# One more step between VectorE's softplus and the triangular products of a stick-breaking head

## The chip, the cores and the metric

The kernel runs on one core of a Trainium2 chip. The metric is the device time of one execution in microseconds (us); lower is better. The engines are TensorE (PE in the trace; PEld is its weight load), VectorE (DVE), ScalarE (ACT), GpSimd (POOL) and SyncE (SP, which here issues most DMAs). Each engine takes its instructions from a queue of its own in the order of the program and waits where data or a buffer is missing.

## The reference

A decoder layer for 512 tokens of width 2048: a mixer with two groups of eight heads each, then a mixture of 32 experts. Group A is sparse attention, group B is stick-breaking attention. What a head of group B computes:

```python
z = einsum('bqhd,bshd->bhqs', q_blk, k)
log_1m = where(strict, log_sigmoid(-z), 0.0)
tail = cumsum(log_1m, axis=3, reverse=True) - log_1m
a = where(strict, exp(log_sigmoid(z) + tail), 0.0)
o = einsum('bhqs,bshd->bqhd', a, v)
```

The outputs of both groups are normed over their heads, concatenated and projected (`w_out`); the result is gated by a modulation vector and added to the residual stream. The experts follow on the normed residual, with the router's two choices per token.

## The kernel before

All weights are streamed from memory. A pool of 23 buffers in SBUF (`big`, tag `b`) serves nearly everything: weight chunks as loaded, their split into a high and a low half (`hl`, ScalarE writes the high half and VectorE, in one stage GpSimd, the low one, L380-L381), modulation rows, heads. Eight banks of PSUM are used as four for the main projections (`mm`) and four for all else (`at`).

The first half of the kernel runs a main stream of projections: for group B the names are B0, B1 (q), B2, B3 (k), B4, B5 (v), two of each with four heads in each; Q0 to Q3 are projections for group A. `steps` (L907) walks a projection in groups of products (`main_b`, L621: six products of 512 columns to a group), and the output projection `main_o` (L966) does the same in six segments O0 to O5; the first two cover group A's heads in the columns 0 and 1, the third is the first that reads group B's.

Everything else is written as generators and put in four lanes (`Lanes`, L49). After each group of main products `tick(rate)` gives every lane `rate` steps in turn (`RATES`, L43: B4, Q2 and Q3 1.2, B5 0.6, segment O0 0.95, segment O1 0.2); a step runs one generator up to its next `yield`. That fixes the order of instructions in every engine's queue: a `yield` issues nothing, it only lets one round of the other lanes and main products come ahead. Where a result is needed, `lanes.until` turns the lanes with no main products between; L1061 does so ahead of the third output segment until group B's norm has been issued.

`stick` (L782) is a head of group B. It works in three blocks of keys, (2,3), (1,) and (0,). A block: the score products into a PSUM bank (L795-L796), step; three activations of ScalarE, |z|, exp, ln (L799-L801), step; VectorE's maximum and sum, the softplus e (L803), step; the triangular products, which add minus the running sums of e to the bank (L806-L811), with GpSimd keeping the total `tot` (L807, L813, L815), step; ScalarE's last exp, which frees the bank (L817), step. That is 15 steps a head. `stick_pv` (L821) multiplies by v later, frees the head's buffer and collects squares for the norm. `sticks` (L844) opens heads as `room` allows: heads 0 to 3 run in lanes 2 and 3 beside B4, Q2 and Q3; heads 4 to 6 start in lanes 3, 0 and 2 at the end of B3 and run beside B5; head 7 follows in lane 3. `norm_o(1)` (L858, L872-L892) is group B's norm: it waits for all heads, adds the squares, sums over partitions with a product (`on`), takes the reciprocal root (`rstd`, L148), and then scales (L888) and splits (ScalarE's high part, L892's low part) the eight heads.

`mod_chunk` (L271) accumulates modulation rows on VectorE (L269, 2.3 us each) between the chunks of weights, and `mod_done` (L330) turns the finished ones with a few products.

Of the kernel before, what the change touches and what calls it, by code (L numbers as in the profile page):

```python
# [75 lines left out]
def tile_hybrid_layer(ctx: ExitStack, tc, A, out, dbg=None):  # L76
# [9 lines left out]
    def slot(shape, dt=F32, name="b"):  # L86
        t = big.tile(shape, dt, name=name, tag="b")
        return t

    def bank(tag, name, dt=F32):  # L90
        t = ps.tile([P, 512], dt, name=name, tag=tag)
        return t
# [3 lines left out]
    def act(o, i, f=AF.Copy, **kw):  # L96
        return SC.activation(o, i, f, **kw)  # L97

    def mm(o, l, r, start, stop, skip=False):
        return T.matmul(o, l, r, start=start, stop=stop, skip_group_check=skip)  # L100
# [681 lines left out]
    def stick(h):  # L782
        g, hh = divmod(h, 4)
        q, k = qb[g], kb[g]
        opened[0] += 1
        buf = slot([P, 1664], name="st")
        tot = buf[:, 1152:1664]
        for js in ((2, 3), (1,), (0,)):
            o = pk[js[0]].start
            at = {j: slice(pk[j].start - o, pk[j].stop - o) for j in js}  # L790
            n = at[js[-1]].stop
            z = bank("at", "z")[:, :n]
            for j in js:
                zj = z[:, at[j]]
                mm(zj, k[:, hh, 128 * j:128 * j + 128], q[:, hh, 128 * j:], j == js[0], False, True)  # L795
                mm(zj[:, 0:128], identb, smaskb, False, False, True)  # L796
            yield
            e = buf[:, o:o + n]
            act(e, z, AF.Abs)  # L799
            act(e, e, AF.Exp, scale=-1.0)  # L800
            act(e, e, AF.Ln, bias=one1)  # L801
            yield
            V.scalar_tensor_tensor(e, z, 0.0, e, op0=OP.max, op1=OP.add)  # L803
            yield
            if js == (2, 3):
                mm(z[:, 128:256], mones, e[:, 256:384], False, False, True)  # L806
                G.tensor_tensor(tot[:, 384:], e[:, 128:256], e[:, 256:384], op=OP.add)  # L807
            else:
                mm(z[:, 128:], mones, tot[:, 128 * js[0] + 128:], False, False, True)
            for j in js:  # L810
                mm(z[:, at[j]], negU, e[:, at[j]], False, j == js[-1], True)  # L811
            if js == (1,):
                G.tensor_tensor(tot[:, 256:], tot[:, 256:], e[:, 128:], op=OP.add)  # L813
            if js[0]:
                G.tensor_copy(tot[:, 128 * js[0]:128 * js[0] + 128], e[:, 0:128])  # L815
            yield
            act(e, z, AF.Exp)  # L817
            yield
        weighed.append((h, buf))
# [24 lines left out]
    def sticks(left=0):  # L844

        while stick_left[0] > left:
            if weighed and vb_done[weighed[0][0] // 4]:
                yield from stick_pv(*weighed.pop(0))
            elif len(todo) > left and opened[0] < room() and kb_done[todo[0] // 4] and qb_done[todo[0] // 4]:
                yield from stick(todo.pop(0))  # L850
            else:
                yield
# [699 lines left out]
```

## Time and profile before

| | us |
|---|---|
| median of 3 runs | 1876.78 |
| lowest, highest | 1874.24, 1879.22 |
| profiled execution | 1876.25 |
| its span, first to last instruction | 1874.4 |

| engine | busy us | share of the span |
|---|---|---|
| TensorE | 1735.2 | 93% |
| VectorE | 938.9 | 50% |
| ScalarE | 507.6 | 27% |
| GpSimd | 153.2 | 8% |

The span is that of one execution on the chip. A row of a timeline gives the start, the duration of the row's instructions (several of one kind are merged, x2) and in brackets how long the engine had stood idle before and what released it. A releaser is inferred from semaphores: it is the last thing that was waited for, not always the first cause.

### The profile page before, as it was taken

What the parts mean: (1) busy time and instruction counts of PE and PEld (TensorE: products, weight loads), DVE (VectorE), ACT (ScalarE), POOL (GpSimd) and SP (SyncE); (2) the same over time, 40 slices, a digit from 0 to 9 for tenths busy, and PEclk for the clock granted to TensorE, in tenths of its full rate; (3) what the DMA queues carried; (4) which work ended last, traced back from release to release, by engine and by line L of the source; (5) the groups of instructions that cost most, each with busy time, mean ns of one, the idle gap of its engine ahead of it and who ended that gap; (6) DMA issues with size and microseconds to landing.
All of it is one profiled execution on the core that took longest, in us unless ns stands there. A gap on an engine that the chain in (4) does not pass through costs nothing.

```text
span 1874.4 us, 20840 instructions
## 1 busy us (share of the span) xinstructions
PE 1735.2 (93%) x8097; PEld 975.6 (52%) x8097; DVE 938.9 (50%) x1518; ACT 507.6 (27%) x960; POOL 153.2 (8%) x116
## 2 busy tenths in 40 slices
PE   6999997999899998998899999999999999999997
PEld 3777775775567676887333333333333333333333
DVE  6798943378955857555334424342434233333425
ACT  4323342555455532321212111121112110211010
POOL 0001010332225110000100000000000000000000
PEclk8999998999999999999999999999999999999999
DMA  9876734312245645669899999999999999999997
GB/s 389 339 279 229 257 125 156 135 68 84 74 138 201 230 179 205 222 225 409 313 412 419 419 420 420 419 419 420 420 419 419 420 419 420 419 420 419 419 413 275
DMA packets 91574, 585.06 MB, mean 312 GB/s; under 512 B 10866, under 2 KB 11034, under 8 KB 27046
## 3 DMA queue, kind: packets, MB, share of 16 engines
q1 hardware_dynamic: 87184, 569.09, 76.0%
q0 software_dynamic: 4288, 14.60, 2.1%
q8 instruction: 65, 1.06, 0.2%
q14 instruction: 37, 0.30, 0.0%
HBM read 583.64 MB, written 8.40 MB: 316 GB/s over the span
## 4 chain that ended last, share of the span: by engine, by line
DMA 41%; PE 36%; DVE 14%; issue 4%; ACT 4%; POOL 1%; SPq 0%; DVEq 0%; ACTq 0%; POOLq 0%
DMA w_u<-in_w_up 15%; DMA w_g<-in_w_gate 12%; DMA w_d<-in_w_down 12%; PE O L100 8%; PE B L100 7%; PE y L100 3%; PE u L100 3%; PE Q L100 2%; PE g L100 2%; PE z L100 2%; DVE accv L269 2%; DVE acc L269 1%; PE cb L100 1%; DVE sel L722 1%; DMA w_m<-in_w_m 1%
## 5 line engine op out<-in xcount | busy, mean ns | idle before, releaser
L100 PE MATMUL u<-w_u,xe 128*64 128x512 f32 x1024 | 267.3, 605 | 22.8 <-DMA w_u<-in_w_up 21.6
L100 PE MATMUL g<-w_g,xe 128*64 128x512 f32 x1024 | 240.8, 596 | 18.2 <-DMA w_g<-in_w_gate 18.0
L1277 DVE TENSOR_TENSOR x<-cb,x 128x512 f32<-128x512 f32 x256 | 157.2, 681 | 186.2 <-PE cb L100 186.2
L100 PE MATMUL y<-w_d,uT 128*64 128x512 f32 x1024 | 236.9, 600 | 0.7 <-ACT uT L97 0.7
L100 PEld LDWEIGHTS u<-w_u,xe 128*64 128x64 f32 x1024 | 78.4, 138 | 200.9 <-issue 137.7
L100 PEld LDWEIGHTS g<-w_g,xe 128*64 128x64 f32 x1024 | 75.9, 137 | 170.5 <-issue 130.7
L269 DVE SCALAR_TENSOR_TENSOR accv<-w_m_None,sil,accv 128x2048 f32<-128x2048 f32 x62 | 150.4, 2426 | 6.7 <-DMA accv<-in_b_gate 6.5
L1267 DVE SCALAR_TENSOR_TENSOR yt<-y,gs,accv 128x512 f32<-128x512 f32 x64 | 47.8, 747 | 200.4 <-PE y L100 200.4
L97 ACT ACTIVATE xe<-ga,modc 128x128 f32<-128x128 f32 x254 | 93.9, 463 | 126.2 <-PE y L100 95.7
L100 PEld LDWEIGHTS y<-w_d,uT 128*64 128x64 f32 x1024 | 66.5, 136 | 116.0 <-issue 107.6
L100 PE MATMUL cb<-yH,oT 128*128 128x512 f32 x256 | 107.7, 421 | 0.9 <-DVE x L1277 0.9
L97 ACT ACTIVATE uT<-uT 128x512 f32<-128x512 f32 x16 | 9.6, 598 | 343.5 <-PE uT L1318 343.5
L100 PE MATMUL cb<-yL,oT 128*128 128x512 f32 x256 | 101.0, 394 | 0.0
L1269 DVE TENSOR_TENSOR yL<-yt,yH 128x512 fp32r<-128x512 f32 x64 | 44.3, 692 | 110.3 <-DMA w_g<-in_w_gate 52.7
L97 ACT ACTIVATE yH<-yt 128x512 fp32r<-128x512 f32 x64 | 40.3, 630 | 204.6 <-DVE yt L1267 121.4
L1219 POOL DMA_INDIRECT xg<-x1d,gi x15 | 15.2, 1014 | 818.7 <-DVE t L1222 597.2
L100 PEld LDWEIGHTS cb<-yH,oT 128*128 128x128 f32 x256 | 48.0, 188 | 49.8 <-issue 38.9
L1241 PEld LDWEIGHTS ga<-cst,xg 128*128 128x128 f32 x252 | 35.2, 209 | 62.9 <-issue 42.0
L97 ACT ACTIVATE hl<-w_B 128x1024 fp32r<-128x1024 f32 x48 | 50.5, 1052 | 54.9 <-DVE accv L269 29.5
L1312 DVE TENSOR_TENSOR u<-sg,u 128x512 f32<-128x512 f32 x16 | 11.0, 688 | 106.0 <-PE u L100 106.0
L381 DVE TENSOR_TENSOR hl<-w_O,hl 128x1024 fp32r<-128x1024 f32 x32 | 39.2, 1229 | 43.6 <-ACT hl L97 28.3
L381 POOL TENSOR_TENSOR hl<-w_B,hl 128x1024 fp32r<-128x1024 f32 x17 | 47.9, 2817 | 142.6 <-ACT hl L97 112.3
(428 smaller groups left out, 2915.4 us busy)
## 6 DMA issues: line engine op xcount, KB each, us to landing
w_g<-in_w_gate SPq DMA_DIRECT2D x128, 1024.0 KB, 19.9
w_u<-in_w_up SPq DMA_DIRECT2D x128, 1024.0 KB, 21.2
w_d<-in_w_down SPq DMA_DIRECT2D x128, 1024.0 KB, 19.9
w_m_None<-in_w_mod SPq DMA_DIRECT2D x64, 1024.0 KB, 4.9
w_m<-in_w_m SPq DMA_DIRECT2D x32, 1024.0 KB, 11.7
w_B<-in_w_b SPq DMA_DIRECT2D x48, 512.0 KB, 4.6
w_O<-in_w_o SPq DMA_DIRECT2D x16, 1024.0 KB, 5.0
w_A<-in_w_a SPq DMA_DIRECT2D x8, 848.0 KB, 11.3
```

The lines of the kernel that those rows point to most:

```text
L97: return SC.activation(o, i, f, **kw)
L100: return T.matmul(o, l, r, start=start, stop=stop, skip_group_check=skip)
L269: V.scalar_tensor_tensor(acc, w, s, acc, op0=OP.mult, op1=OP.add)
L381: low_eng[0].tensor_tensor(t[:, 1], s, t[:, 0].bitcast(F32), op=OP.subtract)
L722: V.match_replace(out=acc, in_to_replace=m8, in_values=acc, imm_value=SEL)
L1219: G.indirect_dma_start(xs, None, x1d[:, :], bass.IndirectOffsetOnAxis(ap=gi[:, 0:1], axis=0), bounds_check=S - 1, oob_is_err=False)
L1241: T.transpose(pb[:, 128 * j:128 * j + 128], xs[:, 512 * c:512 * c + 512].rearrange("p (k j) -> p j k", j=4)[:, j], ident)
L1267: V.scalar_tensor_tensor(yt, y, g, rowv[G2][:, cs], op0=OP.mult, op1=OP.mult)
L1269: V.tensor_tensor(yL[:, cs], yt, yH[:, cs].bitcast(F32), op=OP.subtract)
L1277: return lambda: V.tensor_tensor(acc[q][:, t], pb, acc[q][:, t], op=OP.add)
L1312: V.tensor_tensor(u, sg, pb, op=OP.mult)
```

## The change

Between VectorE's softplus and the triangular products a head yields twice instead of once. No instruction is added, removed or altered; a head has 18 steps instead of 15.

```diff
             act(e, e, AF.Ln, bias=one1)
             yield
             V.scalar_tensor_tensor(e, z, 0.0, e, op0=OP.max, op1=OP.add)
+            yield
             yield
             if js == (2, 3):
                 mm(z[:, 128:256], mones, e[:, 256:384], False, False, True)
```

## Rows read from the trace of the kernel before

**Rows 1.** Page, chain that ended last, shares of the span by engine.

```profile
DMA 41%; PE 36%; DVE 14%; issue 4%; ACT 4%; POOL 1%; SPq 0%; DVEq 0%; ACTq 0%; POOLq 0%
```

**Rows 2.** Stretches: us; busy PE, PEld, DVE, ACT, POOL; clock, DMA share, GB/s.

```profile
245.00:330.00 85.00, 74.41 (x417) 54.96 (x416) 33.46 (x32) 29.41 (x49) 13.36 (x14) 0.94 0.41 141
...
577.00:650.00 73.00, 68.38 (x283) 49.44 (x282) 53.38 (x48) 41.44 (x73) 29.72 (x22) 1.00 0.55 203
650.00:712.30 62.30, 58.91 (x239) 44.79 (x238) 38.78 (x43) 23.01 (x34) 4.76 (x5) 0.97 0.55 206
...
853.00:1874.40 1021.40, 951.72 (x4106) 385.84 (x4104) 361.97 (x700) 164.96 (x376) 23.70 (x24) 0.99 0.99 407
```

**Rows 3.** SyncE: a wait of its queue (us, times, longest); first expert load.

```profile
SPq L247 <- PE O L100: 104.1, 20, 10.1
...
852.98 6.47 SPq L247 DMA_DIRECT2D w_g<-in_w_gate  x6
```

**Rows 4.** TensorE's timeline, heads 0-2: start, us, engine, operation, [idle before <- releaser].

```profile
290.79 1.19 PE L100 MATMUL z<-st,mone 128*128 128x256 f32 x2 [3.79 <-DVE st L803]
...
292.49 1.63 PE L100 MATMUL B<-hl,h2H 128*128 128x512 f32 x2
...
303.70 0.88 PE L100 MATMUL z<-st,mone 128*128 128x384 f32 x2 [2.64 <-DVE st L803]
...
325.03 4.58 PE L100 MATMUL pob<-st,B 128*128 128x128 f32 x16 [2.21 <-ACT B L97]
```

**Rows 5.** ScalarE's timeline, same stretch.

```profile
287.04 1.06 ACT L97 ACTIVATE hl<-w_B 128x1024 fp32r<-128x1024 f32 x1 [8.29 <-PE B L100]
```

**Rows 6.** TensorE's timeline, heads 4-6.

```profile
595.33 1.12 PE L100 MATMUL md<-accv,one 128*128 128x512 f32 x2 [1.59 <-ACT st L97]
...
624.95 0.88 PE L100 MATMUL z<-st,mone 128*128 128x384 f32 x2 [0.52 <-DVE st L803]
...
642.94 0.50 PE L100 MATMUL B<-hl,h3H 128*128 128x512 f32 x1 [1.14 <-DVE hl L381]
```

**Rows 7.** VectorE's timeline, end of B5.

```profile
642.80 0.55 DVE L803 SCALAR_TENSOR_TENSOR st<-z,st 128x384 f32<-128x384 f32 x1
...
643.27 4.81 DVE L269 SCALAR_TENSOR_TENSOR accv<-w_m_None,sil,accv 128x2048 f32<-128x2048 f32 x2
...
650.95 2.36 DVE L381 TENSOR_TENSOR hl<-w_O,hl 128x1024 fp32r<-128x1024 f32 x2 [2.86 <-ACT hl L97]
```

**Rows 8.** Tile of a head: one of ScalarE's activations, ns min/median/max.

```profile
L97 ACT ACTIVATE st<-st,one x24: 614/617/727, 248.1 to 667.0; 128x384 f32<-128x384 f32 x16, 128x512 f32<-128x512 f32 x8
```

**Rows 9.** TensorE's timeline, output projection's first segments.

```profile
650.02 2.42 PE L100 MATMUL pob<-st,B 128*128 128x128 f32 x8
...
651.88 1.03 PE L100 MATMUL O<-hl,o00H 128*128 128x512 f32 x2
...
682.98 1.02 PE L100 MATMUL on<-ssb,one 128*128 128x512 f32 x2
...
688.77 1.19 PE L100 MATMUL O<-hl,o00H 128*128 128x512 f32 x2 [3.38 <-DVE mix L1013]
...
712.23 0.70 PE L100 MATMUL O<-hl,o10H 128*128 128x512 f32 x2
...
719.12 0.49 PE L100 MATMUL O<-hl,o10H 128*128 128x512 f32 x1 [1.18 <-ACT hl L97]
...
720.38 0.50 PE L100 MATMUL O<-hl,o10H 128*128 128x512 f32 x1 [0.77 <-DVE hl L381]
```

**Rows 10.** VectorE's timeline, norm of group B (first and last of five).

```profile
685.42 0.69 DVE L153 SCALAR_TENSOR_TENSOR rt<-on,ro 128x512 f32<-128x512 f32 x1 [3.52 <-ACT ro L97]
...
687.94 0.68 DVE L1013 TENSOR_TENSOR mix<-O,accv 128x512 f32<-128x512 f32 x1
...
694.38 1.40 DVE L888 SCALAR_TENSOR_TENSOR B<-B,vecs,ro 128x512 f32<-128x512 f32 x2
...
697.10 0.68 DVE L892 TENSOR_TENSOR o10L<-B,o10H 128x512 fp32r<-128x512 f32 x1
```

## The prediction

> **What bounds the kernel now.** I read the chain that ended last first. DMA carries 41% of it and TensorE 36% [rows 1]: two regimes, not one. The table of stretches [rows 2] puts the border at 853 us. From there the 16 DMA engines are busy 0.99 of 1021 us: the expert weights set the pace. In the three stretches before it that hold the heads, DMA is busy 0.41 to 0.55, and TensorE is the nearest to full: 74.4 of 85 us while heads 0 to 2 run, 68.4 of 73 while heads 4 to 6 run, 58.9 of 62.3 in the first two segments of the output projection. The stick heads run only in the first half, so the edit can act there alone. Does a shift there reach the end? SyncE's first expert load is issued at 852.98, and what holds its queue in the whole trace is buffers that others give back, 104.1 us behind output products alone [rows 3]. The weights start when the first half lets go of its buffers, so I pass a shift on one to one.
>
> Then I read TensorE's timeline, and beside it ScalarE's and VectorE's, at each place where TensorE stands. Four places matter.
> First, heads 0 to 2: it stands 3.79 and 2.64 us for the softplus (L803), and after the first wait two 512-column products take 1.63 us, at 712.23 only 0.70 [rows 4, 9]. The releaser is not the real cause: ScalarE had held back the split of a weight chunk until 287.04, because that chunk's buffer came free only then [rows 5], and the softplus is queued behind it.
> Second, heads 4 to 6: small waits of 1.59 (a PSUM bank), 0.52 (softplus) and 1.14 (VectorE's half of a split) [rows 6].
> Third, the border between the first two output segments: 3.38 us for VectorE's `mix`, and slow products after it [rows 9].
> Fourth, the border at which the output projection first needs group B's normed result: 712.23 begins the new segment, and the second weight chunk starts at 719.12, standing 1.18 and 0.77 more [rows 9].
>
> **The change part by part.** It adds no instruction. It gives each of 3 blocks of 8 heads one empty step, 24 in all, so it moves everything that these heads issue later past other work in every engine's in-order queue; SyncE's and GpSimd's queues see it as later tile releases and later adds. I counted steps by the rule of `tick`: each group of main products gives each of the four lanes RATES steps, whether it has work or not. A head is 15 steps now and 18 after.
>
> Heads 0 to 3: the projection B4 gives 32 x 1.2 = 38.4 steps to each lane. Two heads in one lane use 30, after the change 36, so they still fit; head 3 then uses Q2 and Q3, and the next users of the lane wait for Q0 anyway. No tail grows here. What changes is the order. Triangular products now come a further 1/1.2 of a main group later, behind about 1.1 us of products that need nothing from the head (a group takes 1.37: the second output segment has 16 in 688.77 to 712.23, 1.5 of it slow pace, below [rows 9]), and head 2 takes its buffer two to three groups later, so the held-back split finds a buffer sooner. The two waits are 6.43 us. They cannot all go: for head 2's second block the split of the following chunk is again ahead of the softplus on ScalarE. I take half, -3.2 us. Bounds: idle in this stretch is 85 - 74.4 = 10.6 us, of which the last 2.2 are evictions that the change does not touch, so -8.4; on the other side head 2's buffer request now stands behind the next chunk's loads, and one more wait like the first would cost 3.8, so about +4.
>
> Heads 4 to 6 start together when B3 is done and must share B5 (32 x 0.6 = 19.2 steps) with the start of head 7. Now head 7 opens after 15 steps, then after 18. The 1.59 wait goes, since the score banks are released just ahead of the gate's products and not after; with it the 0.52 and the 1.14: -3.3 in all. But the first softplus of head 7 moves to the very end of B5, and VectorE has two modulation updates of 2.4 each and the split for the output projection queued behind it. Now that softplus runs at 642.80, the updates until 648.1, and the split at 650.95 is in time [rows 7]. After: counted from the start of B5's last chunk, two groups and a score product (about 0.8) end at 3.5; ScalarE, at 0.62 an instruction [rows 8], is through one eviction and the head's three activations at 6.0; VectorE's maximum ends at 6.6, two updates at 11.4, the low half of the split at 12.6. TensorE's four groups end at 6.3, but its value product waits for two more evictions, to 7.3, takes about 1.9 (650.02 to 651.88, where the first output product starts) [rows 9], to 9.2, and one output product can follow, to 9.4. It stands 3.2. Sum -0.1, bounds -3.3 and +3.2.
>
> Head 7 itself: its lane ends 3 steps later for head 4 and 3 for head 7. Group B's norm (`norm_o(1)`) needs it, and the first two output segments give only 15.2 + 3.2 steps. Before, the loop that waits for the norm ahead of the third segment turned 2 times; after, it turns 8 times, and nearly the whole norm is then issued with no product beside it. Two consequences.
> At the 3.38 wait, `mix` stood on VectorE behind the norm's reciprocal root. That is gone there: -3.4, and with it the slow products. The granted clock of that stretch is 0.97 [rows 2], 1.9 us lost at most in 62.3; I take 1.5. Sum -4.9.
> At the fourth place the norm now stands in full between the segments. After the last product: one `mix` pair 1.4, the sum of the squares 0.7, from the norm's product to the root 2.4 (682.98 to 685.42), the root 2.5 (685.42 to 687.94) [rows 9, 10], in all 7.0; then 16 scalings and differences at 0.68 (five took 694.38 to 697.78 [rows 10]), 10.9; then VectorE's half of the second chunk's split, queued behind them, 1.2 [rows 7], and 0.3 until its ScalarE half has passed it. The second chunk starts 19.4 us after the border. Before it started at 720.38 less one product of 0.23, 7.9 after 712.23. That is +11.5. The first chunk of 5.5 us fits inside and does not shorten it. TensorE stands over 8 us in one piece and comes back slow: +1.5, as in the wait that goes. Sum +13.0. Bounds +8 (VectorE's run overlaps more) and +16 (the norm's four output buffers must wait for loads that now come ahead).
>
> On the clock: the rows show that after standing 3.79 and 3.38 us the engine runs for a while at the lower of its two levels, 1.2 instead of 2.4 GHz [rows 4, 9]. The Trainium skill, "TensorE: Matmul & The Clock Gate", Part 1, says that the throttled state is the default and that sustained work lifts it, so that each restart is paid once whatever the length of the gap. By that rule the long new pause costs no more than each of the shorter ones it replaces; if two such pauses go in the first stretch for one that comes, the sum would be 1.5 us less, 1879.5. No run here shows that yet.
>
> Sum: -3.2 - 0.1 - 4.9 + 13.0 = +4.8 us. The profiled execution took 1876.25 (span 1874.4 and 1.85 around it), 0.5 below the median of 1876.78; I set both equal and predict 1876.25 + 4.8 = 1881.0. What a measurement of this kernel can tell from no change is about 0.3%, 5.6 us: 1871.2 to 1882.4.
>
> **The rivals.** (a) Slower: head 2's buffer. If the split of the fourth weight half of B4 (2,1) still starts after the products of the chunk before it, head 2's softplus stands behind it and TensorE now waits in the middle of a chunk, with no second buffer ahead. The first stretch then gives +4 for -3.2 and the total is +12.0, 1888.2. For it: 23 buffers, all taken there, and ScalarE's 8.29 us wait [rows 5]. Against it: one buffer fewer is held at that moment. It decides from the point at which that split waits more than about 4 us.
> (b) Faster: the waits for the softplus were the real cost, and an added step removes them all, -8.4, with -3.3 in B5 and no stand at the first output product, while the norm's tail costs its lower bound: -8.4 - 3.3 - 4.9 + 8 = -8.6, 1867.7. For it: TensorE does name L803 at the largest waits. Against it: the count of 8 turns, which does not depend on any duration.
> (c) Nothing arrives: what is lost before 853 us is hidden by loads that run anyway, or the moved steps stay under cover: 0, 1876.3. Against it: SyncE's queue waits for TensorE's buffers [rows 3].
>
> **How the numbers follow.** Forecast 0.50, around 1881.0, its own range 1876 to 1886: 0.29 below the 1882.4 border and 0.21 above. (a) 0.18, all slower. (b) 0.20, 0.18 of it faster and 0.02 within the border. (c) 0.12, 0.10 of it within the border and 0.02 faster. So faster 0.20, same 0.41, slower 0.39. The range leaves out a tenth at each end: the outer part of (b) below 1868, and the outer part of (a) and the +16 bound above 1889.
>
> **What would show it.** Right: in the changed kernel TensorE stands some 8 us ahead of the third output segment, on VectorE's scaling, and once more for the split; no wait on `mix` between the first two segments; a wait of about 3 us behind the value product of head 4. The two L803 waits in the first stretch shrink to about half together. Wrong, if the norm has been issued before the third segment, if the first stretch's idle time grows over 10.6 us, or if the first expert load does not move with the shift before it.

## The result and the profile of the changed kernel

| | before | changed |
|---|---|---|
| median, us | 1877.63 (6 runs) | 1900.13 (6 runs) |
| lowest, highest | 1874.24, 1879.96 | 1889.56, 1902.76 |
| profiled execution | 1876.25 | 1902.58 |
| its span | 1874.4 | 1900.8 |

The ratio is 1.0107, with a 95% interval of 1.0087 to 1.0128: the change costs about 20 us. A later set of the same kernel gave 1893.57 (4 runs) and 1.0097 (1.0075 to 1.0120). The forecast of 1881.0 with a range of 1868 to 1889 was too low. The way it went (slower) was in the sum; the size was not.

First the page of the changed kernel: the busy time of the engines, then the chain that ended last.

```profile
PE 1749.6 (92%) x8097; PEld 982.8 (52%) x8097; DVE 941.8 (50%) x1518; ACT 508.1 (27%) x960; POOL 148.3 (8%) x116
...
DMA 41%; PE 25%; DVE 9%; ACT 2%; issue 2%; POOL 1%; SPq 0%; DVEq 0%; ACTq 0%; POOLq 0%
```

The number of TensorE's instructions is what it was, and its busy time rose from 1735.2 to 1749.6: the same products took 14.4 us longer. That is the first surprise, since the forecast looked mainly for waits. (In a second trace of the same kernel, e8_same_again below, it is 1739.2.) DMA has 41% of the chain as before. TensorE's 25% cannot be set against the 36% of [rows 1]: the shares of this chain add up to 80%, those of the one before to 100%, so it was followed back over less of the span.

Seven landmarks in TensorE's timeline, the same products in both kernels, cut the first half into six legs. The second trace of the changed kernel is that of the run e8_same_again below.

| leg, us | before | changed | changed, second trace | forecast of the change |
|---|---|---|---|---|
| first score product to the value product of head 0 | 79.04 | 83.78 | 78.58 | -3.2 |
| to the first index product (head 3, beside Q2 and Q3) | 38.87 | 45.06 | 43.40 | 0 |
| to the first score product of heads 4 to 6 | 211.19 | 214.25 | 211.93 | 0 |
| to the first output product (B5) | 76.79 | 74.55 | 74.56 | -3.3 |
| to the end of the second output segment | 60.32 | 60.35 | 58.74 | -1.7 (+3.2 - 4.9) |
| to the third segment's first product with `o11` (border and norm) | 13.5 | 28.03 | 27.99 | +13.0 |
| sum | 479.7 | 506.0 | 495.2 | +4.8 |

The sums differ by 26.3 and 15.5 us, and the shift reaches the end. SyncE issues the first expert loads, eight in a row, from 847.76 in the kernel before and from 874.27 in the changed one, 26.5 later, and the span is 26.4 longer. (The 852.98 of [rows 3], which the prediction takes for the first load, is the start of the last six of these eight.) SyncE's timeline, before and changed:

```profile
847.76 11.69 SPq L247 DMA_DIRECT2D w_g<-in_w_gate  x8
```

```profile
874.27 11.69 SPq L247 DMA_DIRECT2D w_g<-in_w_gate  x8
```

In this trace two legs carry most of the loss that the forecast did not have, the first and the second; the second trace has it in the second leg alone (+4.5 us). The table of stretches shows them (us from the start; length; busy PE, PEld, DVE, ACT, POOL with counts; granted clock; DMA share; GB/s). The first two rows are those legs, the third is the projection B5, the fourth the first two output segments, the fifth the border behind them, the last the experts; they answer [rows 2].

```profile
246.21:329.99 83.78, 72.96 (x393) 52.84 (x391) 33.77 (x32) 28.64 (x47) 13.50 (x14) 0.88 0.39 134
329.99:375.05 45.06, 42.07 (x160) 30.16 (x161) 13.61 (x10) 18.81 (x31) 9.71 (x7) 0.92 0.36 124
...
589.30:661.99 72.69, 68.53 (x288) 49.82 (x286) 49.58 (x47) 43.12 (x75) 24.11 (x20) 1.00 0.59 212
663.85:724.20 60.35, 57.79 (x238) 44.24 (x236) 32.49 (x30) 16.15 (x24) 5.46 (x7) 0.97 0.54 203
724.20:752.23 28.03, 17.15 (x52) 12.28 (x51) 23.34 (x29) 11.33 (x15) 2.31 (x2) 0.76 0.23 76
874.30:1900.80 1026.50, 956.64 (x4129) 389.97 (x4127) 367.26 (x704) 166.26 (x377) 23.70 (x24) 0.99 0.99 407
```

In the first leg TensorE stands 83.78 - 72.96 = 10.8 us; before it was 79.04 - 68.45 = 10.6. The waits did not shrink in sum, and 393 products took 73.0 us and not 68.4 (394 products), at a granted clock of 0.88 and not 0.94. In the second leg it stands 3.0 us, before 0.2, and the clock is 0.92, before 1.00.

TensorE's timeline of these two legs answers [rows 4]:

```profile
276.17 1.62 PE L100 MATMUL z<-st,mone 128*128 128x384 f32 x2 [2.81 <-DVE st L803]
...
302.32 0.73 PE L100 MATMUL z<-st,mone 128*128 128x256 f32 x2 [3.61 <-DVE st L803]
...
319.86 1.49 PE L100 MATMUL z<-st,mone 128*128 128x384 f32 x2
...
329.99 6.27 PE L100 MATMUL pob<-st,B 128*128 128x128 f32 x16 [2.65 <-ACT B L97]
...
356.97 0.76 PE L100 MATMUL z<-st,mone 128*128 128x256 f32 x2 [2.30 <-DVE st L803]
```

The columns tell the block: 256 is a head's middle block, 384 its last. Both waits of [rows 4] are head 2's. Its middle block, which waited 3.79, now waits 3.61 (at 302.32); its last block, which waited 2.64, no longer waits (at 319.86). A new wait of 2.81 stands ahead of them, in the last block of heads 0 and 1, and behind it two products of 384 columns take 1.62, which took 0.88 behind the wait of 2.64 before [rows 4]: 1.2 and not 2.4 GHz. The sixteen value products of heads 0 and 1 take 6.27, before 4.58. At head 3 a wait of 0.22 in the middle block became 2.30.

What holds the softplus is on VectorE. Here are its rows at the new wait in heads 0 and 1 and at the one in head 3:

```profile
274.20 1.23 DVE L381 TENSOR_TENSOR hl<-w_B,hl 128x1024 fp32r<-128x1024 f32 x1 [5.46 <-ACT hl L97]
275.34 1.28 DVE L803 SCALAR_TENSOR_TENSOR st<-z,st 128x512 f32<-128x512 f32 x2
...
355.13 1.23 DVE L381 TENSOR_TENSOR hl<-w_Q,hl 128x1024 fp32r<-128x1024 f32 x1 [4.72 <-ACT hl L97]
356.27 0.55 DVE L803 SCALAR_TENSOR_TENSOR st<-z,st 128x384 f32<-128x384 f32 x1
```

Each time the softplus (the row `st<-z,st`) stands directly behind the low half of a weight chunk's split (`hl<-w_B,hl`), and that split waits 5.46 and 4.72 us for ScalarE, whose half of the split is queued behind the head's activations. The added steps moved these blocks so that a chunk begins between their activations and their softplus. In the kernel before no block of heads 0 to 3 stood so. There the softplus of heads 0 and 1 in their last block came ahead of that chunk's split (VectorE, kernel before):

```profile
269.72 0.69 DVE L803 SCALAR_TENSOR_TENSOR st<-z,st 128x512 f32<-128x512 f32 x1 [1.23 <-ACT st L97]
...
272.58 1.22 DVE L381 TENSOR_TENSOR hl<-w_B,hl 128x1024 fp32r<-128x1024 f32 x1
```

The buffer that the forecast looked at did come free sooner, but by 2.1 us only: ScalarE's split of that chunk starts 39.0 us after the first score product, before 41.1. ScalarE stands 0.79 us ahead of it where it stood 8.29 [rows 5] mainly because the last exponentials of heads 0 and 1 now fall into that time. And head 2's middle block no longer stands behind this split but behind the next chunk's, which waits 7.30. ScalarE's timeline of the two:

```profile
285.18 1.06 ACT L97 ACTIVATE hl<-w_B 128x1024 fp32r<-128x1024 f32 x1 [0.79 <-PE B L100]
...
298.94 1.06 ACT L97 ACTIVATE hl<-w_B 128x1024 fp32r<-128x1024 f32 x1 [7.30 <-DVE accv L269]
```

The border at the third output segment went as the forecast drew it. TensorE's timeline answers [rows 9] and VectorE's [rows 10]; of VectorE's norm these are the sum of the squares, the first scaling, the last difference and the split:

```profile
667.21 0.50 PE L100 MATMUL O<-hl,o00H 128*128 128x512 f32 x1 [2.56 <-DVE hl L381]
...
726.63 1.10 PE L100 MATMUL on<-ssb,one 128*128 128x512 f32 x2 [2.24 <-DVE ssb L873]
...
733.26 1.22 PE L100 MATMUL O<-hl,o10H 128*128 128x512 f32 x2 [5.53 <-ACT o10H L97]
...
742.89 0.62 PE L100 MATMUL O<-hl,o10H 128*128 128x512 f32 x1 [2.48 <-ACT hl L97]
744.15 0.80 PE L100 MATMUL O<-hl,o10H 128*128 128x512 f32 x1 [0.64 <-DVE hl L381]
```

```profile
725.80 0.68 DVE L873 TENSOR_TENSOR ssb<-ssb,ssb 128x512 f32<-128x512 f32 x1
...
731.79 1.41 DVE L889 SCALAR_TENSOR_TENSOR B<-B,vecs,ro 128x512 f32<-128x512 f32 x2
...
741.14 1.47 DVE L893 TENSOR_TENSOR o11L<-B,o11H 128x512 fp32r<-128x512 f32 x2
...
742.87 1.23 DVE L381 TENSOR_TENSOR hl<-w_O,hl 128x1024 fp32r<-128x1024 f32 x1 [0.25 <-ACT hl L97]
```

The last product of the second segment ends at 724.20. The first scaling starts 7.6 us later (forecast 7.0), the sixteen operations take 10.8 (10.9), and the second chunk starts 19.9 behind the border (19.4), before 8.2. With the slow products behind it the leg costs 14.5 (13.0).

### The profile page after: what moved, and what is told of

It reads as the page before. It is cut to its first block, busy times and chain, and to the rows that moved or that the text cites. A ratio compares the mean times of both kernels' runs of the same rounds, so it can differ in the third digit from the quotient of the medians.

```text
span 1900.8 us, 20836 instructions
## 1 busy us (share of the span) xinstructions
PE 1749.6 (92%) x8097; PEld 982.8 (52%) x8097; DVE 941.8 (50%) x1518; ACT 508.1 (27%) x960; POOL 148.3 (8%) x116
## 4 chain that ended last, share of the span: by engine, by line
DMA 41%; PE 25%; DVE 9%; ACT 2%; issue 2%; POOL 1%; SPq 0%; DVEq 0%; ACTq 0%; POOLq 0%
DMA w_u<-in_w_up 15%; DMA w_g<-in_w_gate 13%; DMA w_d<-in_w_down 13%; PE O L100 9%; PE y L100 3%; PE B L100 2%; PE u L100 2%; PE g L100 2%; PE Q L100 2%; DVE sel L707 1%; DVE sel L722 1%; PE cb L100 1%; DVE accv L269 1%; DVE m L721 1%; PE z L100 1%
## 6 DMA issues: line engine op xcount, KB each, us to landing
w_g<-in_w_gate SPq DMA_DIRECT2D x128, 1024.0 KB, 19.9
w_d<-in_w_down SPq DMA_DIRECT2D x128, 1024.0 KB, 19.9
```

## Experiments

### The extra step for some heads alone

> The extra step for heads 0 to 3 only. In the profiled run of the changed kernel TensorE is 5.0 us late at the value product of head 0 (329.99 against 325.03), 11.1 late after head 3 (411.08 against 399.93) and 14.2 late when heads 4 to 6 begin (589.30 against 575.09); all else of the 26.4 comes behind that. Theory 'two places' (the first half loses by itself where a head's activations and its softplus fall on the two sides of a weight chunk's split, and the shift reaches the end): about +14 in a profiled run, 1886 to 1892. Rival 'one place' (the early loss is taken up by waits for weights before the experts begin, and nearly all of the loss is the norm of group B): +0 to +4, 1876 to 1881.

```diff
             V.scalar_tensor_tensor(e, z, 0.0, e, op0=OP.max, op1=OP.add)
             yield
-            yield
+            if h < 4:
+                yield
```

> The extra step for heads 4 to 7 only; the order of the first stretch is then that of the kernel before. Theory 'two places': from the start of heads 4 to 6 on, the changed kernel gained 2.2 us in B5, lost 3.2 at the first output product, gained about 4 between the first two output segments and lost 14.5 on the norm of group B, so about +12 in all, 1886 to 1891; the two parts then add up to the whole. Rival 'one place': nearly the whole loss, +18 to +23, 1895 to 1900. A third reading, by the forecast's own sum for this part (-0.1 -4.9 +13.0): +8, 1884.

```diff
-            yield
+            if h >= 4:
+                yield
```

> The extra step for head 7 alone. Half of the late steps: the loop ahead of the third output segment then turns 5 times, but the sum of the squares, the norm's product and its root are issued beside output products, and only the 16 scalings and differences are left alone between the segments. Theory 'what stands alone is paid, not the number of steps' (16 by 0.68 is 10.9, then 1.4 for a mix pair and 1.5 for the split: the second weight chunk starts 13.8 us after the border and not 7.9, and the wait for mix between the first two segments, 3.4 with 1.5 of slow products, goes): +1 to +3, 1877 to 1879. Rival 'every late step costs alike' (half of the +10 that heads 4 to 7 cost): +5, 1881.

```diff
-            yield
+            if h == 7:
+                yield
```

| | median, us (runs) | ratio, 95% interval | shift at heads 4 to 6 | shift behind the norm |
|---|---|---|---|---|
| heads 0 to 3 | 1884.24 (10) | 1.0040, 1.0026 to 1.0053 | +10.9 | +10.9 |
| heads 4 to 7 | 1885.69 (9) | 1.0050, 1.0035 to 1.0065 | 0.0 | +10.5 |
| head 7 | 1877.58 (10) | 1.0009, 0.9998 to 1.0020 | +0.9 | +2.4 |

Against before in the same sets (1875.83, 1875.83, 1875.34) these are +8.4, +9.9 and +2.2. Two places it is: the first two add up to 18.3, near the whole, and a shift of 10.9 at heads 4 to 6 stands unchanged behind the norm and gives a span 9.5 us longer. The early loss is not taken up by anything. Both medians lie under the lowest that was expected (1886), by 1.8 and 0.3. For heads 4 to 7 the interval is +6.6 to +12.2 us, so this run does not tell the forecast's own +8 for that part from the +10 and more of the theory.

Head 7 alone settles what in the norm costs. Its second weight chunk starts 13.7 us behind the border (expected 13.8), and with the sum of squares and the root under cover the whole is +2.2; in its trace the first two output segments take 56.3 us and not 60.3, since the wait for `mix` has gone (forecast for that term -4.9). It is not the number of late steps that is paid, but what of the norm is left with no product beside it. This is TensorE's timeline in that kernel at the border:

```profile
721.49 0.50 PE L100 MATMUL O<-hl,o10H 128*128 128x512 f32 x1 [0.98 <-ACT hl L97]
722.75 0.50 PE L100 MATMUL O<-hl,o10H 128*128 128x512 f32 x1 [0.76 <-DVE hl L381]
```

### The softplus ahead of the split

> All heads have their 18 steps, and the triangular products stay where the change put them. Only in three blocks, the last of heads 0 and 1 and the second of head 3, the softplus is issued together with the activations, one step earlier, so that it stands ahead of the next chunk's split in VectorE's queue and not behind it. Theory 'place in the queue': the waits of 2.81 us at 276.17 and 2.30 us at 356.97 go, and with each the slow products behind it, so TensorE is 6 to 9 us earlier after head 3 than in the changed kernel, and the end is 1890 to 1895 against 1900. Rival 'held longer' (the cost is that a head keeps its PSUM bank and its buffer a step longer, wherever its softplus stands): no change, 1899 to 1901.

```diff
             act(e, e, AF.Ln, bias=one1)
-            yield
+            early = js == (0,) if h < 2 else (h, js) == (3, (1,))
+            if not early:
+                yield
             V.scalar_tensor_tensor(e, z, 0.0, e, op0=OP.max, op1=OP.add)
+            if early:
+                yield
             yield
             yield
```

1887.62 (6 runs), 1.0056 (1.0039 to 1.0072): 12.5 us under the changed kernel's first set, 6.0 under its second, and earlier than expected. The wait at 276 is gone, the one at head 3 is back at 0.22. On VectorE the two softplus now come ahead of the split, which no longer waits:

```profile
268.90 0.69 DVE L805 SCALAR_TENSOR_TENSOR st<-z,st 128x512 f32<-128x512 f32 x1 [4.31 <-ACT st L97]
270.81 0.69 DVE L805 SCALAR_TENSOR_TENSOR st<-z,st 128x512 f32<-128x512 f32 x1 [1.21 <-ACT st L97]
271.42 2.34 DVE L269 SCALAR_TENSOR_TENSOR accv<-w_m_None,sil,accv 128x2048 f32<-128x2048 f32 x1
273.68 1.22 DVE L381 TENSOR_TENSOR hl<-w_B,hl 128x1024 fp32r<-128x1024 f32 x1
```

The first two legs take 77.3 and 39.7 us, the second 5.4 less than in the changed kernel and 0.8 more than before; the first three together take 328.2, before 329.1. Head 2's own wait of 3.60 is still there. All 18 steps are there, the buffer and the bank are held as long, and the products stand where the change put them. So what the first half paid for is the place of three softplus instructions in VectorE's queue. The rival falls.

### The added step elsewhere in the block

> The added step stands at the end of each block, behind the last exponential, and not between the softplus and the products. A head has 18 steps as in the changed kernel and every score product, activation and softplus keeps the place that the change gave it; only the triangular products and the last exponential come one step earlier. Theory 'place in the queue': nothing is gained; the first wait of the first stretch grows from 2.81 by about the group of 1.4 us that no longer comes ahead of the products, the last wait of head 3 likewise, and the end is 1892 to 1903. Rival 'distance' (the step costs because the products come later): the loss of the first half goes and only that of the norm stays, 1884 to 1888.

```diff
             V.scalar_tensor_tensor(e, z, 0.0, e, op0=OP.max, op1=OP.add)
             yield
-            yield
...
             act(e, z, AF.Exp)
             yield
+            yield
```

> The added step stands ahead of the softplus: the triangular products stay where the change put them, and every softplus comes a step later. Theory 'place in the queue': three more blocks have a chunk's split between activations and softplus (the second of heads 0 and 1, the first or the last of heads 2 and 3), each with a wait of 1 to 3 us on the softplus, so the end is 3 to 8 us behind the changed kernel: 1897 to 1908. Rival 'number of steps' (18 steps cost what they cost, wherever the added one stands): 1892 to 1901, as the changed kernel.

```diff
             act(e, e, AF.Ln, bias=one1)
             yield
+            yield
             V.scalar_tensor_tensor(e, z, 0.0, e, op0=OP.max, op1=OP.add)
             yield
-            yield
```

At the end of the block: 1899.30 (4 runs), 1.0107 (1.0090 to 1.0124), as the changed kernel. Distance between softplus and products is not the cost. The two waits of head 3 grew by the group that no longer comes ahead, from 2.30 to 3.66 and from 0.68 to 2.03, and in heads 4 to 6 one of 1.65 became 4.71; the first of the first stretch shrank from 2.81 to 1.80, which was not expected and is not explained here.

Ahead of the softplus: 1904.52 (4 runs), 1.0133 (1.0109 to 1.0157), 4.4 us behind the changed kernel's first set and 11 behind its second. Where a chunk now begins ahead of the softplus the waits stand as expected or larger, in heads 4 to 6 too (3.30 and 5.30):

```profile
263.26 0.67 PE L100 MATMUL z<-st,mone 128*128 128x256 f32 x2 [1.61 <-DVE st L804]
...
319.12 1.62 PE L100 MATMUL z<-st,mone 128*128 128x384 f32 x2 [4.44 <-DVE st L804]
...
603.74 0.49 PE L100 MATMUL z<-st,mone 128*128 128x128 f32 x2 [3.30 <-DVE st L804]
...
651.56 1.62 PE L100 MATMUL z<-st,mone 128*128 128x384 f32 x2 [5.30 <-DVE st L804]
```

The number of steps does not set the time: the same 18 steps give 1887.6, 1893.6 to 1900.1, 1899.3 or 1904.5, as the softplus falls on one side or the other.

### The norm beside output products

> The extra step for all heads, and the rate of the second output segment raised from 0.2 to 0.6, so that its 16 groups give each lane 9.6 steps and not 3.2: all but one turn of group B's norm is issued beside output products. Theory 'the norm stands alone' (TensorE waits 2.24, 5.53, 2.48 and 0.64 us around the norm, 19 us from the last product of one segment to the second chunk of the next, and is slow after it): about 11 to 14 us come back, 1886 to 1890. Rival 'hidden' (the third segment would have waited for its weights anyway): no change, 1898 to 1902.

```diff
-RATES = (1.2, 1.4, 1.1, 1.5, 0.6, 0.95, 0.2, 0.8, 0.65)
+RATES = (1.2, 1.4, 1.1, 1.5, 0.6, 0.95, 0.6, 0.8, 0.65)
```

1892.44 (4 runs), 1.0081 (1.0055 to 1.0108): between the expected 1886 to 1890 and the rival's 1898 to 1902, and only 1.1 under the changed kernel's second set. The legs are the better test. From the first output product to the products of `o11` the legs take 82.1 us, in the changed kernel 88.4, before 73.8: 6.3 come back and not 11 to 14. TensorE no longer waits for the norm but for `mix`, which VectorE has queued behind the norm's operations:

```profile
727.48 1.19 PE L100 MATMUL O<-hl,o10H 128*128 128x512 f32 x2 [8.10 <-DVE mix L1014]
```

```profile
725.27 1.47 DVE L893 TENSOR_TENSOR o11L<-B,o11H 128x512 fp32r<-128x512 f32 x2
726.65 0.68 DVE L1014 TENSOR_TENSOR mix<-O,accv 128x512 f32<-128x512 f32 x1
```

So the norm's work on VectorE is what stands in the way; issued beside the products, more than half of the wait only moves to another of VectorE's instructions.

### What holds the second wait

> The changed kernel without the bias of the two gate rows: no fill by GpSimd and no load of the bias row stand ahead of a gate row's first update, and the two rows are computed without it. It leaves that bias out of the result. Theory 'the second wait of the first stretch is not the heads' own' (in the changed kernel the first update of a gate row waits 6.69 us for that load, the split of the next weight chunk waits for the update's buffer, and the head's activations and softplus are queued behind the split; the step moved the head but not this): the wait of 3.61 us at 302.32 goes and the slow products behind it, so TensorE is 4 to 6 us earlier at the value product of head 0, and the end is 1894 to 1897 against 1900. Rival 'the step itself' (the softplus is late because the head runs late): no change, 1899 to 1901.

```diff
-                if v in (G1, G2):
-                    G.memset(accs[v], 0.0)
-                    G.dma_start(accs[v][0:1], A["b_gate"][int(v == G2):int(v == G2) + 1])
-            gemv(accs[v], w, sil[:, q:q + 1], q == 0 and v not in (G1, G2))
+            gemv(accs[v], w, sil[:, q:q + 1], q == 0)
```

> The kernel before (15 steps a head) with only two heads open at a time until four are done, so head 2 takes no buffer while the projection B4 runs; it opens with head 3 behind the value products of heads 0 and 1. Leaving the bias row out did not take the second wait away (3.41 us in place of 3.61): the split then waited for a product of TensorE. Theory 'buffers' (the splits of the weight chunks wait for one of 23 buffers, and head 2's is the one too many): in the first stretch no wait on the softplus of over 1 us is left, TensorE's idle time between the first score product and the value product of head 0 falls from 10.6 to 4 to 6 us, and that value product comes 10 to 14 us earlier (6 to 8 of it are head 2's own products, which move behind it). Rival 'loads' (the chunk or the modulation row has not landed): the splits wait as long, the idle time stays at 8 to 11 us. The end is not the test, since heads 2 and 3 then run on both sides of the splits in the query projections: 1870 to 1885.

```diff
-ROOM = (3, 3, 4)
+ROOM = (2, 3, 4)
```

The bias row was not it: 1898.95 (4 runs), 1.0119 (1.0097 to 1.0141), and the wait is 3.41 for 3.61. But the split that stands ahead of the softplus on ScalarE now names a product as its releaser, in place of VectorE's update; that is, it waits for the buffer that this product still read:

```profile
296.54 1.06 ACT L97 ACTIVATE hl<-w_B 128x1024 fp32r<-128x1024 f32 x1 [7.08 <-PE B L100]
```

With two heads open at a time the first stretch has no wait on a softplus left. TensorE stands 63.54 - 61.17 = 2.4 us in it (expected 4 to 6, before 10.6), and the value product of head 0 comes 16.0 us earlier (expected 10 to 14). The stretch to that product, and TensorE's timeline of what follows:

```profile
245.50:309.04 63.54, 61.17 (x367) 46.72 (x365) 31.38 (x29) 22.74 (x35) 9.74 (x10) 0.95 0.47 165
```

```profile
309.04 4.58 PE L100 MATMUL pob<-st,B 128*128 128x128 f32 x16 [0.69 <-ACT B L97]
...
334.36 1.19 PE L100 MATMUL z<-st,mone 128*128 128x256 f32 x2 [4.70 <-DVE st L803]
...
348.62 0.88 PE L100 MATMUL z<-st,mone 128*128 128x384 f32 x2 [1.78 <-DVE st L803]
```

The idle time fell as the theory said, but its reason does not hold: on ScalarE the splits wait for a product's buffer as long as before, with no head 2 there to take one.

```profile
289.35 1.06 ACT L97 ACTIVATE hl<-w_B 128x1024 fp32r<-128x1024 f32 x1 [9.82 <-PE B L100]
...
298.88 1.06 ACT L97 ACTIVATE hl<-w_B 128x1024 fp32r<-128x1024 f32 x1 [8.48 <-PE B L100]
```

These waits of 9.82 and 8.48 us cost TensorE little (it stands 0.77 us for each split): a split follows TensorE's products by design, since it takes the buffer that they give back. What costs is a head's block queued behind it, and with head 2 gone there is none. Whether one buffer more would shorten the second wait was not separated by this run. And the 16 us are given back: heads 2 and 3 then run side by side, stand 4.70 and 1.78 for their softplus, and the first index product starts at 363.00, before 363.90. The whole is 1876.28 against 1878.24 (9 and 12 runs), 0.9977 (0.9958 to 0.9996), an interval that ends just under 1.

### The same kernel again

> The changed kernel itself once more, for a second trace of it. Two of the runs so far that have its order in the first stretch stood idle as long as it there (11.0 us), but the stretch was 91.5 and 89.9 us long and not 95.0. Theory 'the clock, not the waits, varies': idle time of the first stretch again 10.8 to 11.1 us, with its length between 89 and 95 us as the granted clock goes (0.87 to 0.92), and the end 1890 to 1902. Rival 'fixed': 95 us again and 1900 to 1903.

1893.57 (4 runs), 1.0097 (1.0075 to 1.0120). Five traces share the order of instructions in the first leg: the two of the changed kernel, those with the step in heads 0 to 3, with the other rate and without the bias row. These are the stretches of three of them, with the second trace of the changed kernel first:

```profile
245.73:324.31 78.58, 67.17 (x394) 49.44 (x392) 33.77 (x32) 28.66 (x47) 13.51 (x14) 0.96 0.38 134
```

```profile
244.99:325.58 80.59, 69.60 (x393) 51.41 (x391) 33.77 (x32) 28.65 (x47) 13.52 (x14) 0.92 0.38 132
```

```profile
246.29:328.21 81.92, 70.89 (x394) 52.02 (x392) 33.76 (x32) 28.62 (x47) 13.48 (x14) 0.90 0.37 130
```

TensorE stands 11.4, 11.0 and 11.0 us, in the changed kernel's first trace 10.8: the idle time is fixed by the order, within 0.6 us (expected up to 11.1, so a little more). The clock of 0.96 in the second trace is above the 0.87 to 0.92 that was expected. The busy time of the same 393 or 394 products is 67.2, 69.6, 70.9 and 73.0, as the granted clock is 0.96, 0.92, 0.90 and 0.88. The first wait shows how: it is 2.81 us in both traces of the changed kernel, and behind it the pair of 384 columns takes 1.62 in the first and 0.88 in the second:

```profile
275.69 0.88 PE L100 MATMUL z<-st,mone 128*128 128x384 f32 x2 [2.81 <-DVE st L803]
```

Three traces have the old order in this leg (the kernel before, heads 4 to 7, head 7): 79.0, 79.0 and 78.5 us, with 10.6 to 10.9 us of idle time and a clock of 0.94 to 0.96. So the two orders stand idle nearly alike. The new one was slowed more in four of its five traces, and in one it was not.

### Two attempts at a kernel that beats both

> An attempt at a kernel that beats both: the extra step for heads 0 to 3 only, with the softplus of three blocks ahead of the next chunk's split as in the third run; heads 4 to 7 with their 15 steps; the rate of the second output segment 0.3 and not 0.2, so that the loop ahead of the third segment does not turn at all. From the third run's trace its first half ends 2.1 us earlier than before at head 4 (1.0 of it already there at the first head). Theory 'place in the queue and the norm alone' gives -1 to -2 for the heads and -1 to -3 for the norm: 1871 to 1874. Rival 'VectorE at the border' (the norm beside the second segment holds up mix at its end, as the fourth run showed with 8.10 us): +1 to +4, 1877 to 1880.

```diff
-RATES = (1.2, 1.4, 1.1, 1.5, 0.6, 0.95, 0.2, 0.8, 0.65)
+RATES = (1.2, 1.4, 1.1, 1.5, 0.6, 0.95, 0.3, 0.8, 0.65)
...
             act(e, e, AF.Ln, bias=one1)
-            yield
+            early = js == (0,) if h < 2 else (h, js) == (3, (1,))
+            if not early:
+                yield
             V.scalar_tensor_tensor(e, z, 0.0, e, op0=OP.max, op1=OP.add)
+            if early:
+                yield
             yield
-            yield
+            if h < 4:
+                yield
```

> A last attempt at a kernel that beats both: two heads open at a time as in the ninth run, with 15 steps, but the middle block of heads 2 and 3 takes the added step between softplus and products, and the softplus of head 3's last block stands with its activations, so that no chunk's split stands between them. In the ninth run the first stretch gained 16.0 us at the value product of head 0, and heads 2 and 3 gave it back, 7.6 of it as two waits for the softplus (4.70 and 1.78) and the slow products behind them, the rest as their own products. Theory 'distance pays where no split lies between': the wait of 4.70 shrinks to about 3.1 (one more group of products comes ahead), the one of 1.78 goes, and the end is 2 to 5 us earlier than before: 1871 to 1874. Rival 'given back later': the shorter waits only start the sparse heads of group A earlier, which wait for their own softmax; 1875 to 1878.

```diff
-ROOM = (3, 3, 4)
+ROOM = (2, 3, 4)
...
             act(e, e, AF.Ln, bias=one1)
-            yield
+            early = (h, js) == (3, (0,))
+            if not early:
+                yield
             V.scalar_tensor_tensor(e, z, 0.0, e, op0=OP.max, op1=OP.add)
+            if early:
+                yield
             yield
+            if h in (2, 3) and js == (1,):
+                yield
```

The first diff is against the changed kernel, the second against the kernel before. Neither beats the kernel before: 1877.83 (12 runs), 1.0006 (0.9993 to 1.0019), and 1876.61 (12 runs), 0.9997 (0.9984 to 1.0010). In the first one the heads gain 0.9 and the norm 0.3; with 2.1 that were there at the first score product the products of `o11` come 3.3 us earlier, and 1.8 of these are lost again before the first expert load. `mix` held up the third segment by 0.58 only, so the rival has the time right and not the reason. In the second one the wait of 4.70 fell to 2.36, but the one of 1.78 in the last block, which was to go, grew to 3.53:

```profile
330.37 0.67 PE L100 MATMUL z<-st,mone 128*128 128x256 f32 x2 [2.36 <-DVE st L805]
...
346.34 1.62 PE L100 MATMUL z<-st,mone 128*128 128x384 f32 x2 [3.53 <-DVE st L805]
```

From the first score product to the first index product it takes 117.9 us in the kernel before and 117.5, 117.3, 117.0 and 116.9 in four kernels that are ordered differently there (two open, two open with one step, the first attempt, and the softplus ahead). In two further traces with the old order it takes 117.9 and 119.1, so these differences say little. What sets this time was not looked for.

## Why the prediction was wrong

**Heads 0 to 2: -3.2 forecast, -0.5 and +4.7 measured.** This step failed, and twice. The term itself, half of two waits that add up to 6.43 us, came out: head 2's middle block waits 3.61 behind the following chunk's split, as the forecast said, and its last block no longer waits, -2.8. What the forecast put at nothing is the other heads: the step moved the last block of heads 0 and 1 over the beginning of the next chunk, and a new wait of 2.81 arose there that took the gain back. So the idle time stayed at 10.8 to 11.4, before 10.6, which the prediction had named as a sign that it was wrong. The wait that is left in head 2 stayed without the bias row and went only when head 2 did. The second failure is the clock: the forecast put a price on slow products only at the two output borders. In this leg alone they are worth between -1.3 and +4.5 us of busy time against the kernel before. The upper bound of +4 was worked out for one more wait like the first; that the +4.7 of one trace lies near it is luck.

**Head 3: 0 forecast, +4.5 and +6.2 measured.** This is the step that failed most clearly. "No tail grows here. What changes is the order" was its sentence; the order of this head was then not followed through, block by block, against the chunks of Q2 and Q3. With the softplus of one block put ahead of the split, +0.8 is left. The runs showed that directly.

**Between head 3 and heads 4 to 6: 0 forecast, +0.7 and +3.1 measured.** In the changed kernel's two traces it is idle time, 16.5 and 17.9 us for 15.1; the waits that grew are among those of group A's heads for ScalarE, and why they did is open. In the trace with the step in heads 0 to 3 alone it is slow products: 15.3 us idle, but 199.2 us busy for 196.1. There 7 us run at half speed though TensorE did not stand in them:

```profile
395.00:402.00 7.00, 7.00 (x23) 5.80 (x22) 2.93 (x11) 2.39 (x5) 1.92 (x1) 0.51 0.00 0
```

**Heads 4 to 6: -0.1 forecast, about +0.3 measured.** B5 gained 2.2 (forecast 3.3). Of the three waits [rows 6] 1.59 became 0.91 and 1.14 went, but 0.52 grew to 1.65: the last block of head 4 got a chunk's split between its activations and its softplus, as in the first half, and here five operations of group A's norm behind the split as well. Of the 2.2 us, 1.8 are head 7's products that moved behind (busy 70.3 before, 68.5 after). The stand at the first output product is 2.56, where 3.2 was forecast; in the first trace slow products follow it, in the second none.

**The border of the first two output segments: -4.9 forecast.** The wait for `mix` is gone, and where nothing else changed (head 7 alone) the leg is 4.1 us shorter: right, and 0.8 too large. In the changed kernel the whole leg, with the stand at its beginning, is 0.0 and -1.6, for -1.7.

**The norm: +13.0 forecast, +14.5 measured in the changed kernel and +12.7 with heads 4 to 7 alone.** The mechanism was right: the whole norm stands between the segments, as the count of eight turns implies (the trace does not show the turns themselves), and the sums of VectorE's operations held to within 0.6 us each. The difference is the slow products: 2.7 us in the changed kernel, 1.5 forecast.

**The shift to the end, one to one.** Right: +10.9 behind the norm for heads 0 to 3 gave a span 9.5 longer, +26.5 in the changed kernel gave 26.4. The prediction's 852.98 for the first expert load should be 847.76; nothing in its sum hangs on it.

So the part of heads 4 to 7, forecast at +8.0, measured +10.5; the part of heads 0 to 3, forecast at -3.2, measured +10.9 in a trace and +8.4 in the median. Rival (a) had the right sign for the first stretch. Its condition did not come (the split that it names waits 0.79 us, not more than 4); what it describes came one chunk later, where the split waits 7.30, and cost head 2's middle block no more than before. Rivals (b) and (c) fell: the waits did not go, and the shift arrived. The bounds of the range were made for waits and the norm; head 3 and the slow products of the first half were in none of them.

Of the clock the forecast took from the Trainium skill, "TensorE: Matmul & The Clock Gate", Part 1, that the throttled state is the default and sustained work lifts it, and concluded that each restart is paid once, whatever the length of the pause. The runs do not bear that out as a price per pause: the same pause of 2.81 us was paid in one trace and not in another, and 7 us were slow with no pause. The same part of the Trainium skill says that the activity is judged over a window which runs on by itself and does not begin with the program, so that one kernel comes out differently from run to run. With that the traces agree: the first leg of the changed kernel had a granted clock of 0.88 in one trace and of 0.96 in the other.

## What to carry to other kernels

A yield changes no instruction, but it moves each later one past what other lanes put into the in-order queues; follow every block of every generator against the borders where a chunk's split is issued, and look for pairs (activation, softplus) that fall on its two sides. Ask of each wait what holds the instruction that is named, and what holds that: here the softplus, the split, and the products whose buffer the split takes over: a wait that hurts nobody until something is queued behind it. Price a new pause of TensorE at its length plus, as an estimate from these runs, 0 to some 3 us of slow products (none behind one wait of 2.81, 2.7 behind the norm), and put that spread into the range.

## What was not expected of the hardware

The same order of instructions, with idle time alike within 0.6 us, took 78.6, 80.6, 81.9, 81.9 and 83.8 us in five traces, by a granted clock of 0.88 to 0.96: TensorE's busy time is no constant of a kernel. And it ran at 0.51 from 395 to 402 us in the trace with the step in heads 0 to 3, with no idle time at all. Eight products of one column each stand three times just ahead of it and once in it, among products of 512 columns; in the second trace of the changed kernel the same products went at 1.00.
